# A two-layer attention and feed-forward trunk on one core: products moved behind the conditioning transposes, a table copied by heads, row loads shifted, two small additions moved

## The chip, the core and the metric

The kernel runs on one core of a Trainium2 chip. A core has five engines with a queue each: PE (TensorE, the matrix unit, with PEld as its weight loads), DVE (VectorE), ACT (ScalarE), POOL (GpSimd) and SP (SyncE), which here issues all data transfers. Each engine takes its queue in order; the engines wait for one another by semaphores. Matmul results go to PSUM, eight banks of 2 KB in each of 128 partitions; everything else lies in SBUF. The metric is the device time of one launch in microseconds (us).

## The reference, cut to what matters

One inference step for 1024 prompt rows and 8 groups of 16 sample rows (1152 rows, width 1024), all in float32. Layer 0 has windowed attention with a sink per head and a T5 bias; its output stream gives one key and value projection, which layer 1 uses in banded attention with a bias clipped by distance. Each sub-layer is modulated by a conditioning vector and closed by a LayerNorm.

```
for l in range(2):
    sh_m, sc_m, g_m, sh_f, sc_f, g_f = split(silu(c) @ w_ada[l] + b_ada[l], 6)
    h = x * (1 + sc_m) + sh_m
    if l == 0:
        q, k, v = split(h @ w_qkv_a)              # 16 heads, 4 of keys
        m = max(max(s), sink); e = exp(s - m)     # s = q k / 8 + t5 bias, in the window
        p = e / (sum(e) + exp(sink - m))
    else:
        q = h @ w_q_b                             # k, v: from the stream after layer 0
        p = softmax(q k / 8 + relclip bias)       # band of 9 chunks
    x = LN(ALPHA * x + (1 + g_m) * (p v @ w_o))
    u = (x * (1 + sc_f) + sh_f) @ w_up            # 1024 -> 5632, causal convolution of width 3
    x = LN(ALPHA * x + (1 + g_f) * ((gelu(g) * a) @ w_down))
    if l == 0:
        k_b, v_b = split((x * (1 + sc_kv) + sh_kv) @ w_kv_b)
```

Outputs are the stream, the new keys and values, and the last convolution rows.

## The kernel before

Float32 precision comes from splitting: each operand is held as a rounded high part and the rest as a low part, and each product is three matmuls (low by high, high by low, high by high). `split` (L165, L176) makes the two parts: a cast on ACT, a subtraction on DVE or POOL. `wload` issues the load of a weight block (L180) and splits it into a ring `wring` of four slots `(wh, wl)`, of which attention uses two. `HX` holds the split activations.

The code is written in program order, and a scheduler in the framework orders each engine's queue when the kernel is built, by its own model of the costs; `issue_after(i)` keeps what stands under it from being ordered ahead of the instruction i. So a small edit can reorder whole stages.

The stages of the profile: the opening with the key projections (0 to 70 us), attention 0 (to 420), out projection 0 (to 550), up projection 0 (to 1071), down projection 0 (to 1375), keys and values for layer 1 (to 1570), attention 1 (to 1930), out projection 1 (to 2091), up 1 (to 2560), down 1 (to 2780), and the last norms.

*Opening* (`opening`). The conditioning product has two halves h of 512 columns: 32 matmuls L249 for each, with the weight `adaw` loaded in eight pieces a half; L262 adds the bias, L265 transposes, L268 to L271 copy the result as scale G and shift B. Then each half of x (`x1in`, three blocks of 384 rows) is modulated (L278 on DVE, L280 on ACT), split into HX, and multiplied with the matching half of two key weights, `wk[0]` and `wk[1]` (`mmT`, L376, 12 matmuls for a block, half and weight, 144 in all), which sum up in banks 0 to 5. `tables` makes the T5 table (L1421 on PE, L1422 on DVE, L1423 to DRAM as `ea`), and `skew(0)` copies it into `ska` (L1441), from which shifted bias rows are read (L541, L602).

*Attention.* Scores (L624, L627), softmax (L590 to L603), transposes of the probabilities into a bank of a ring `tbk` of two (L650), whose result ACT casts (L655) and DVE subtracts from (L656), then values (L669 to L681). `sums` makes the row sums of a pair of heads: in layer 0 an exponential of sink minus maximum (L690, ACT), an addition (L691, DVE), a reciprocal (L692), a transpose into a bank of the same ring (L694) and a copy (L695). `item_scores` does the same for sample rows (L769, L770). POOL multiplies (L706) and makes the low parts of weights (L176). For layer 1 `load_hm` loads nine tiles of the stream, modulates them on ACT (L895) and splits them, as input of the query weights (`qload`, `qblock`, L376).

*Down projection* (`down_phase`). 1152 rows are done in three groups of three tiles. For each group a loop over 22 steps j loads one block of the down weight (`in_wdn`, 0.5 MB, L180) and 384 columns of the stored activation (`actD`, L1365), and does 18 matmuls of 512 columns (L1329). Beside the steps, `consts(j)` loads in the first group what the closing norms need: norm rows (L910), gates (L904, L906), and in layer 0 also the second bias table (`tables_b`, to DRAM as `eb`) and `skew(1)`, which copies it 16 x 128 times, shifted, into `skb` (L1441). `resid` loads a tile of the residual stream (L996) at three steps of each group.

## Time and profile before

| | us |
|---|---|
| three runs | 2854.53, 2857.62, 2864.55 |
| median | 2857.62 |
| profiled execution | 2855.29 |
| its span | 2853.2 |

The profile is of one execution; its span runs from the first to the last instruction seen. In a row of the timeline or the chain stand the start, the duration, the engine, the line (L12 is line 12), the operation with output and input, a count, and in brackets the idle time of the engine before it and what ended that. In a row of windows stand, after the stretch, the busy time of PE, PEld, DVE, ACT and POOL with counts, the granted TensorE clock (1.00 is full), the share of the DMA engines in use and their GB/s.

The clock and the transfers over the span, in 40 slices of 71 us:

```profile
PEclk9999989999999999999999999999999999999999
DMA  8655432343444449766785466683232222238652
GB/s 319 186 146 176 112 123 105 102 137 128 140 142 147 143 138 295 250 199 215 264 284 172 121 152 184 172 254 104 89 102 73 70 81 78 77 116 271 224 202 77
```

The digits are tenths. Transfers are heaviest in the opening and in the two down projections (slices 16 to 20 and 37 to 39).

### The profile page before, as it was taken

To read this page: it belongs to the slowest core of one execution; us is meant where nothing else is said; L and a number is where in the kernel's file an instruction comes from. 1 tells how busy PE (TensorE), PEld (TensorE's weight loads), DVE (VectorE), ACT (ScalarE), POOL (GpSimd) and SP (SyncE) were. 2 spreads that over 40 slices of the span, in tenths; PEclk is the share of its full clock that TensorE was granted. 3 is DMA by queue.
4 is the path that set the end of the run, shared out by engine and by line. 5 is a ranking of instruction groups with operands and counts; after the bars stand their busy time and mean duration, and the time that the engine had idled before them with its cause. 6 is when DMAs were issued, how large, how long until landed. Compare 5 with 4: busy or idle time off the path is not lost.

```text
span 2853.2 us, 48907 instructions
## 1 busy us (share of the span) xinstructions
PE 2718.7 (95%) x18086; PEld 2429.6 (85%) x18086; DVE 1681.1 (59%) x3846; ACT 1405.6 (49%) x2996; POOL 1065.2 (37%) x1086
## 2 busy tenths in 40 slices
PE   7998889899999999899999999988999999999998
PEld 5986668899899998788999888866799999997886
DVE  4465657755555555665312677764876555566764
ACT  3465543554444443545424666663455545554441
POOL 0122336676565540000550121131877666630000
PEclk9999989999999999999999999999999999999999
DMA  8655432343444449766785466683232222238652
GB/s 319 186 146 176 112 123 105 102 137 128 140 142 147 143 138 295 250 199 215 264 284 172 121 152 184 172 254 104 89 102 73 70 81 78 77 116 271 224 202 77
DMA packets 215631, 454.48 MB, mean 159 GB/s; under 512 B 39040, under 2 KB 115024, under 8 KB 215392
## 3 DMA queue, kind: packets, MB, share of 16 engines
q1 hardware_dynamic: 215392, 451.35, 49.5%
q8 instruction: 143, 2.34, 0.3%
q14 instruction: 96, 0.79, 0.1%
HBM read 359.40 MB, written 101.30 MB: 161 GB/s over the span
## 4 chain that ended last, share of the span: by engine, by line
PE 64%; DVE 6%; issue 6%; DMA 5%; POOL 2%; ACT 2%; SPq 0%; POOLq 0%; DVEq 0%; ACTq 0%
PE PS L1178 33%; PE PS L1329 15%; PE PS L376 7%; PE PS L388 2%; PE PS L669 1%; PE PS L311 1%; PE PS L650 1%; DMA ws<-in_wdn_dram 1%; POOL HX L176 1%; DMA ws<-in_wo_dram 1%; PE PS L624 1%; DVE F L590 1%; PE PS L627 1%; DVE HX L176 0%; DVE x1att L176 0%
## 5 line engine op out<-in xcount | busy, mean ns | idle before, releaser
L176 POOL TENSOR_TENSOR wl<-ws,wh 128x512 fp32r<-128x512 f32 (+1 forms) x217 | 324.8, 1501 | 649.6 <-ACT wh L165 618.8
L1232 DVE SCALAR_TENSOR_TENSOR PS<-F,PS 128x512 f32<-128x512 f32 (+2 forms) x704 | 348.1, 515 | 141.0 <-ACT PS L1239 62.6
L1178 PE MATMUL PS<-HX,wh 128*128 128x288 f32 x2616 | 402.6, 297 | 12.7 <-DVE F L1027 10.9
L165 ACT CAST wh<-ws 128x512 fp32r<-128x512 f32 (+1 forms) x321 | 244.9, 768 | 316.6 <-PE PS L1329 91.1
L1178 PEld LDWEIGHTS PS<-HX,wh 128*128 128x128 f32 x2616 | 365.7, 189 | 21.4 <-DVE F L1027 11.4
L1329 PE MATMUL PS<-wh,HX 128*128 128x512 f32 x1164 | 363.8, 391 | 8.3 <-DVE HX L176 8.3
L1329 PEld LDWEIGHTS PS<-wh,HX 128*128 128x128 f32 x1164 | 218.9, 188 | 54.4 <-DVE HX L176 9.2
L1178 PE MATMUL PS<-HX,wl 128*128 128x288 f32 x1536 | 253.8, 297 | 0.5 <-ACT F L1202 0.5
L376 PE MATMUL PS<-HX,wh 128*128 128x384 f32 x1248 | 244.6, 339 | 0.0
L1329 PE MATMUL PS<-wl,HX 128*128 128x512 f32 x582 | 227.3, 391 | 0.6 <-DVE wl L176 0.6
L1178 PEld LDWEIGHTS PS<-HX,wl 128*128 128x128 f32 x1536 | 220.0, 188 | 7.1 <-issue 6.2
L376 PEld LDWEIGHTS PS<-HX,wh 128*128 128x128 f32 x1248 | 217.6, 189 | 3.9 <-issue 1.8
L388 PE MATMUL PS<-wh,HX 128*128 128x256 f32 (+1 forms) x936 | 172.0, 314 | 14.6 <-ACT wh L165 7.8
L1178 PE MATMUL PS<-x1att,wh 128*128 128x288 f32 x1168 | 182.2, 297 | 1.6 <-DVE x1att L176 1.6
L1239 ACT ACTIVATE PS<-F 128x512 f32<-128x512 f32 x176 | 138.1, 785 | 74.5 <-DVE F L1211 61.9
L165 ACT CAST HX<-F 128x384 fp32r<-128x384 f32 (+3 forms) x232 | 135.3, 602 | 74.8 <-PE PS L1329 15.6
L1178 PEld LDWEIGHTS PS<-x1att,wh 128*128 128x128 f32 x1168 | 163.9, 188 | 7.0 <-issue 4.9
L706 POOL TENSOR_TENSOR F<-F,gatt 64x512 f32<-64x512 f32 x62 | 79.4, 1281 | 234.9 <-DVE F L681 199.0
L176 DVE TENSOR_TENSOR HX<-F,HX 128x384 fp32r<-128x384 f32 (+3 forms) x188 | 135.4, 731 | 39.1 <-ACT HX L165 36.5
L388 PEld LDWEIGHTS PS<-wh,HX 128*128 128x128 f32 x936 | 135.9, 194 | 25.7 <-ACT wh L165 8.3
L1329 PE MATMUL PS<-HX 128*128 128x512 f32 x630 | 147.7, 394 | 4.8 <-ACT HX L165 4.8
L376 PE MATMUL PS<-HX,wl 128*128 128x384 f32 x624 | 133.4, 351 | 14.5 <-DVE HX L167 8.7
(244 smaller groups left out, 5517.9 us busy)
## 6 DMA issues: line engine op xcount, KB each, us to landing
F<-in_adaw_dram SPq DMA_DIRECT2D x112, 512.0 KB
ws<-in_wup_dram SPq DMA_DIRECT2D x92, 512.0 KB
ws<-in_wdn_dram SPq DMA_DIRECT2D x88, 512.0 KB
actD<-F SPq DMA_DIRECT2D x44, 576.0 KB
F<-actD SPq DMA_DIRECT2D x132, 192.0 KB
F<-in_wdn_dram SPq DMA_DIRECT2D x44, 512.0 KB
x1att<-kH SPq DMA_DIRECT2D x60, 256.0 KB
xd<-F SPq DMA_DIRECT2D x27, 512.0 KB
```

What stands on the lines that cost most here:

```text
L165: self.lastact = nc.scalar.copy(out, in_).ins
L176: self.eng(el).tensor_sub(lo, src, hi.bitcast(F32))
L311: mm = nc.tensor.matmul(ps[32 * j : 32 * j + 32, hf * 256 : hf * 256 + 256], self.cT[:, k * 32 : k * 32 + 32], w[n][:, j * 256 : j * 256 + ...
L376: self.nc.tensor.matmul(out, w[a][:, k * 128 : k * 128 + 128], self.Hx(p, k, s0, n), start=i == 0, stop=i == 23)
L388: self.nc.tensor.matmul(out[:, 0:n], H[:, t0 // 128, p, j * kn + k, :], w[a][:, k * n : k * n + n], start=i == 0, stop=i == 23,)
L590: nc.vector.tensor_tensor_reduce(out=p[:, c0 : c0 + w], in0=ps, in1=b, scale=1.0, scalar=init, op0=ALU.add, op1=ALU.min, accum_out=nm)
L624: mm = nc.tensor.matmul(o, q, khi[a][:, kc], start=first, stop=False, **kw)
L706: self.eng("v" if last else "p").tensor_mul(on[r, q], on[r, q], rb[r, :])
L1178: nc.tensor.matmul(out, w[f][a][:, k * 128 : k * 128 + 128], x[:, k, :], start=start and i == 0, stop=i == 11, skip_group_check=True,)
L1232: nc.vector.scalar_tensor_tensor(o, v, w(i), o, op0=ALU.mult, op1=ALU.add)
L1239: nc.scalar.activation(yp, u[:, bl, 2:258], AF.Identity, bias=w(3), scale=w(2))
L1329: nc.tensor.matmul(ps, h[p][:, i * 128 : i * 128 + 128], w[q][:, hf * 512 : hf * 512 + 512], start=j == 0 and k == 0, stop=j == NFF - 1 an ...
```

## The change

Five edits. (1) In the opening the 36 matmuls of the first half with `wk[1]` are no longer written beside those of `wk[0]`, but behind the second half's transposes, with `issue_after` on the last of these. (2) In layer 1 the ring of two weight slots and the load of the first query weight are put ahead of `load_hm`, and the splits of tiles 4 to 8 there are kept behind that weight's cast. (3) In `sums` the bank is taken at the start, the exponential goes into columns 128 to 131 of it, and the addition reads it from there. (4) In `item_scores` the addition is an activation with bias on ACT. (5) In `down_phase` the steps of `consts` are shifted by 2 (layer 0) or 5 (layer 1), the residual rows are loaded at steps 10, 12 and 14, and the skewed table is copied head by head, one at each of the first 16 steps of the second group.

```diff
@@ -262,7 +262,7 @@
             nc.vector.tensor_add(row[:, cs], ps[:, cs], row[:, 512 + 256 * h : 768 + 256 * h])
             for c in range(2):
                 o = (2 * h + c) * 128
-                nc.tensor.transpose(pt[:, o : o + 128], row[:, o : o + 128], self.ident)
+                tr = nc.tensor.transpose(pt[:, o : o + 128], row[:, o : o + 128], self.ident)
             src = pt[:, cs].rearrange("p (c v j r) -> p v j c r", c=2, v=2, j=2)
             for v in range(2):
                 nc.vector.tensor_copy(aT[:, v, h], src[:, v, :, :, 0:9])
@@ -282,8 +282,15 @@
                     )
                     e = "a" if c % 3 == 2 else "v"
                     self.split(self.tiles(x3[:, c, :]), self.Hx(0, c, s0, w), self.Hx(1, c, s0, w), e, "v")
-                for c in range(2):
-                    self.mmT(wk[c], self.bank(3 * c + bi), s0, w, h)
+                if h == 0:
+                    self.mmT(wk[0], self.bank(bi), s0, w, 0)
+                elif bi == 0:
+                    with self.tc.issue_after(tr.ins):
+                        for b, (z0, z) in enumerate(BLK):
+                            self.mmT(wk[1], self.bank(3 + b), z0, z, 0)
+                if h:
+                    for c in range(2):
+                        self.mmT(wk[c], self.bank(3 * c + bi), s0, w, 1)
         return wk
 
     def ada(self, gi, bank, ring):
@@ -506,6 +513,11 @@
             return 8 * (c // 4) + 4 * a + c % 4 if l == 0 else 2 * c + a
 
 
+        qw = {}
+
+        def qload(c):
+            qw[c] = self.wload(I[("wq0", "wq1")[l]][c])
+
         kvb = Ring(list(SB[l]))
         ka = Arena(self.F, (9504, 0)[l])
         kvt = Ring([(self.X2[:, i * 768 : i * 768 + 768], ka.take(384)) for i in (0, 3, 1, 4)])
@@ -526,9 +538,12 @@
             self.rescale(8, zr)
             for q in range(1, 4):
                 self.vproj(1, q, kvb, kvt)
+            self.wring = Ring(self.wslots[0:2])
+            qload(0)
             self.load_hm(Ring([pall[:, i * 1024 : i * 1024 + 1024] for i in range(3)]), self.affine(4, (8, 9), 1))
 
-        self.wring = Ring(self.wslots[0:2])
+        if l == 0:
+            self.wring = Ring(self.wslots[0:2])
         sbt = []
         base = E[0:1, :]
         for p in range(2):
@@ -577,11 +592,6 @@
                 nc.vector.scalar_tensor_tensor(
                     qs(c, a, o, s0, m), src, -SCALE, hi.bitcast(F32), op0=ALU.mult, op1=ALU.subtract
                 )
-
-        qw = {}
-
-        def qload(c):
-            qw[c] = self.wload(I[("wq0", "wq1")[l]][c])
 
         def softmax(pieces, p, n, sink, nm, rs):
 
@@ -686,11 +696,11 @@
 
             hh = 2 * x.head.c + x.head.a
             cs = slice(hh * 8 + 2 * x.g - 2, hh * 8 + 2 * x.g + 2)
+            t = self.bank(tbk.next())
             if l == 0:
-                nc.scalar.activation(M[:, cs], M[:, cs], AF.Exp, bias=self.sinkH[:, hh : hh + 1])
-                nc.vector.tensor_add(L[:, cs], L[:, cs], M[:, cs])
+                nc.scalar.activation(t[:, 128:132], M[:, cs], AF.Exp, bias=self.sinkH[:, hh : hh + 1])
+                nc.vector.tensor_add(L[:, cs], L[:, cs], t[:, 128:132])
             nc.vector.reciprocal(L[:, cs], L[:, cs])
-            t = self.bank(tbk.next())
             nc.tensor.transpose(t[0:4, 0:128], L[:, cs], self.ident)
             nc.vector.tensor_copy(rl[0:4, :], t[0:4, 0:128])
             q0 = (x.g // 2) * 512
@@ -767,7 +777,7 @@
             if l == 0:
                 e = self.sm.next()[:, 0:1]
                 nc.scalar.activation(e, sink, AF.Exp, bias=nm, scale=-1.0)
-                nc.vector.tensor_add(rs, rs, e)
+                nc.scalar.activation(rs, e, AF.Identity, bias=rs)
             nc.vector.reciprocal(rs, rs)
 
         nk = P0 // 128
@@ -839,7 +849,8 @@
 
         for a in range(2):
             kload(0, a)
-        qload(0)
+        if l == 0:
+            qload(0)
         for bi in range(3):
             qblock(0, bi, qw[0])
         items = [item(p, s) for p in range(2) for s in range(8)]
@@ -884,7 +895,7 @@
         self.nc.sync.dma_start(self.xd[1][t * 128 : t * 128 + 128, :], z)
 
     def load_hm(self, ring, aff):
-        nc = self.nc
+        nc, lead = self.nc, self.lastact
         G, B = aff
         for t in range(NT):
             s = ring.next()
@@ -895,7 +906,10 @@
                     nc.scalar.activation(s3[:, c, :], s3[:, c, :], AF.Identity, bias=B[:, c, 0:1], scale=G[:, c, 0:1])
             else:
                 self.sample_affine(s3, s3, G, B, 0, 8, "v")
-            self.split(s3, self.H[:, t, 0], self.H[:, t, 1], "a", "v")
+            with ExitStack() as es:
+                if t >= 4:
+                    es.enter_context(self.tc.issue_after(lead))
+                self.split(s3, self.H[:, t, 0], self.H[:, t, 1], "a", "v")
 
 
     def ln_gate(self, l, i, smp):
@@ -1367,8 +1381,11 @@
             self.split(r, *h, "a", "v")
             return w, h
 
+        late = 5 if last else 2
+
         def consts(j):
             nonlocal aff
+            j -= late
             if j in (2, 3):
                 self.ln_row(l, 0, j - 2, (ga, ba)[j - 2])
             elif j == 5:
@@ -1380,10 +1397,8 @@
                 self.ln_gate(l, 1, j == 8)
             elif j in (10, 11):
                 self.ln_row(l, 1, j - 10, (self.lng, self.lnb)[j - 10])
-            elif j == 12 and not last:
+            elif j == 13 and not last:
                 self.tables_b(F[0:16, 2048:3072], F[0:16, 3072:4096])
-            elif j == 14 and not last:
-                self.skew(1)
 
         for g, ts in enumerate(GRP):
             final = g == len(GRP) - 1
@@ -1396,7 +1411,9 @@
                 with self.tc.issue_after(self.lastload), self.tc.issue_after(self.lastact):
                     if g == 0:
                         consts(j)
-                    if j in (6, 10, 14):
+                    elif g == 1 and not last and j < 16:
+                        self.skew(1, j, 1)
+                    if j in (10, 12, 14):
                         xs.append(resid(ts[len(xs)]))
                 if todo and j % 4 == 3:
                     finish(*todo.pop(0))
@@ -1435,11 +1452,12 @@
         nc.scalar.copy(t[:, 0:511], t[:, 511:512].to_broadcast([16, 511]))
         nc.sync.dma_start(self.eb, t)
 
-    def skew(self, l):
+    def skew(self, l, h=0, n=16):
         e, sk, w = ((self.ea, self.ska, 384), (self.eb, self.skb, 768))[l]
-        src = e[0:1, :]
+        src = e[h : h + 1, :]
         self.nc.sync.dma_start(
-            sk.rearrange("h (q w) -> h q w", w=w), bass.AP(src.tensor, src.offset, [[w, 16], [0, 128], [1, w]])
+            sk[h : h + n].rearrange("h (q w) -> h q w", w=w),
+            bass.AP(src.tensor, src.offset, [[w, n], [0, 128], [1, w]]),
         )
 
     def build(self):
```

In the opening, PE's queue before, from the first half's products (L376) to the second half's conditioning product (L249), its transposes (L265), the table's product (L1421) and the second half's first products:

```order
L376 MATMUL PS<-HX,wl 128x384 x4
L376 MATMUL PS<-HX,wh 128x384 x8
L376 MATMUL PS<-HX,wl 128x384 x4
L376 MATMUL PS<-HX,wh 128x384 x16
L376 MATMUL PS<-HX,wl 128x384 x4
L376 MATMUL PS<-HX,wh 128x384 x8
L249 MATMUL PS<-F,C 32x256 x20
L265 MATMUL PS<-C,F 128x128 x2
L1421 MATMUL PS<-F 16x384
L376 MATMUL PS<-HX,wl 128x384 x9
```

And PE's queue at the same place after the change (L383 is L376 there, L1438 is L1421):

```order
L383 MATMUL PS<-HX,wh 128x384
L249 MATMUL PS<-F,C 32x256 x4
L383 MATMUL PS<-HX,wh 128x384 x7
L249 MATMUL PS<-F,C 32x256 x16
L265 MATMUL PS<-C,F 128x128 x2
L383 MATMUL PS<-HX,wl 128x384 x4
L383 MATMUL PS<-HX,wh 128x384 x8
L383 MATMUL PS<-HX,wl 128x384 x4
L383 MATMUL PS<-HX,wh 128x384 x8
L383 MATMUL PS<-HX,wl 128x384 x4
L383 MATMUL PS<-HX,wh 128x384 x8
L383 MATMUL PS<-HX,wl 128x384 x7
```

Before, 44 products stand right ahead of the last 20 L249; after, eight of them are still ahead or between, and the 36 of the second key weight follow the transposes.

In down 0, SP's queue before, at the end of the first group (`ws` and `F` take the weight's blocks, `actD` the activation):

```order
L1436 DMA eb<-F 16x768
L1365 DMA F<-actD 128x384
L180 DMA ws<-in_wdn_dram 128x1024
L1365 DMA F<-actD 128x384
L1441 DMA skb<-eb 2048x1x768
L180 DMA F<-in_wdn_dram 128x1024
L1365 DMA F<-actD 128x384
L180 DMA ws<-in_wdn_dram 128x1024
L1365 DMA F<-actD 128x384
```

And SP's queue after the change, in the second group (L1379 is L1365 there, L1458 is L1441):

```order
L180 DMA ws<-in_wdn_dram 128x1024
L1379 DMA F<-actD 128x384
L1458 DMA skb<-eb 128x1x768
L180 DMA F<-in_wdn_dram 128x1024
L1379 DMA F<-actD 128x384
L1458 DMA skb<-eb 128x1x768
L180 DMA ws<-in_wdn_dram 128x1024
L1379 DMA F<-actD 128x384
L1458 DMA skb<-eb 128x1x768
L180 DMA ws<-in_wdn_dram 128x1024
```

One transfer of 2048 rows of 768 has become 16 of 128 rows, each behind one step's two loads; the others follow in the same way.

In down 1, SP's queue before, ahead of the first steps' loads (`x1dn` takes rows; `xd` is the residual stream, `gd` the gates):

```order
L180 DMA ws<-in_wdn_dram 128x1024
L996 DMA x1dn_24120<-xd_95 128x1024
L906 DMA x1dn_24120<-gd 128x1024
L904 DMA x1dn_24120<-gd 128x1x1024
L180 DMA F<-in_wdn_dram 128x1024
L1254 DMA out_conv_dram<-F 128x198
L1365 DMA F<-actD 128x384
L996 DMA x1dn_24120<-xd_95 128x1024
L180 DMA ws<-in_wdn_dram 128x1024
L1365 DMA F<-actD 128x384
L180 DMA ws<-in_wdn_dram 128x1024
```

And SP's queue after it (L1010 is L996, L920 is L906, L1268 is L1254):

```order
L180 DMA ws<-in_wdn_dram 128x1024
L180 DMA F<-in_wdn_dram 128x1024
L1268 DMA out_conv_dram<-F 128x198
L1379 DMA F<-actD 128x384
L1010 DMA x1dn_24135<-xd_95 128x1024
L180 DMA ws<-in_wdn_dram 128x1024
L1379 DMA F<-actD 128x384
L920 DMA x1dn_24135<-gd 128x1024
L1010 DMA x1dn_24135<-xd_95 128x1024
L180 DMA ws<-in_wdn_dram 128x1024
L180 DMA F<-in_wdn_dram 128x1024
```

The two gate loads (L906, L904) and one of the two residual rows no longer stand ahead of the second weight load into `ws` here; one residual row does, and a gate and the other row come behind it.

## The prediction

> **What bounds the kernel now.** I read the page first: the busy shares and the chain that ended last.
>
> ```profile
> PE 2718.7 (95%) x18086; PEld 2429.6 (85%) x18086; DVE 1681.1 (59%) x3846; ACT 1405.6 (49%) x2996; POOL 1065.2 (37%) x1086
> ...
> PE 64%; DVE 6%; issue 6%; DMA 5%; POOL 2%; ACT 2%; SPq 0%; POOLq 0%; DVEq 0%; ACTq 0%
> ```
>
> TensorE (PE) is busy 95% of 2853.2 us, so no stage can be made much shorter by an engine other than PE. The diff adds and removes no matmul. What it can win is part of the 134 us in which PE is idle, and of the time in which PE runs at a lower granted clock after an idle. So I looked for the PE gaps next to the edits, in the timeline, and asked of each gap what ended it.
>
> **Opening.** The timeline of PE, with DVE and SP where they matter, and three windows (us; PE, PEld, DVE, ACT, POOL busy; granted clock; DMA share; GB/s):
>
> ```profile
> 33.87 0.62 PE L249 MATMUL PS<-F,C 128*32 128x256 f32 x2
> 37.13 2.79 PEld L376 LDWEIGHTS PS<-HX,wh 128*128 128x128 f32 x16
> 42.25 2.37 PE L249 MATMUL PS<-F,C 128*32 128x256 f32 x40
> 44.68 0.42 DVE L262 TENSOR_TENSOR F<-PS,F 128x256 f32<-128x256 f32 x1 [12.18 <-PE PS L249]
> 45.98 0.81 PE L1421 MATMUL PS<-F 32*16 32x384 f32 x2 [0.39 <-DVE C L268]
> 48.50 1.01 PE L376 MATMUL PS<-HX,wl 128*128 128x384 f32 x2 [1.70 <-DVE HX L167]
> 48.92 0.64 SPq L1441 DMA_DIRECT2D ska<-ea  x1
> 59.47 0.54 DVE L176 TENSOR_TENSOR HX<-x1in,HX 128x384 fp32r<-128x384 f32 x1
> 59.82 7.61 PE L376 MATMUL PS<-HX,wh 128*128 128x384 f32 x43
> 63.24 1.42 SPq L541 DMA_DIRECT2D F<-ska  x2
> 81.91 0.89 SPq L602 DMA_DIRECT2D F<-ska  x2
> 106.88 0.22 PE L624 MATMUL PS<-x1att 128*128 128x128 f32 x1
> ...
> 0.00:38.00 38.00, 24.74 (x139) 13.09 (x140) 16.63 (x32) 11.79 (x19) 3.08 (x7) 1.00 0.97 377
> 48.00:60.00 12.00, 8.58 (x31) 7.06 (x32) 12.00 (x23) 8.17 (x15) 0.00 (x0) 0.61 0.83 253
> 70.00:120.00 50.00, 49.90 (x367) 48.33 (x366) 13.65 (x43) 17.15 (x47) 7.75 (x7) 1.00 0.68 206
> ```
>
> The second half's 20 conditioning products (L249, the row counts each twice, x40) stand behind 44 L376 products and start at 42.25; their sum is taken by L262 at 44.68. Everything of the second half of x hangs on that: from 48 to 60 PE works 8.58 of 12 us at clock 0.61, while DVE is busy all 12. The data were there long before: 377 GB/s for 38 us are 14.3 MB, which is all that is requested up to there (two halves of the conditioning weight 8.39 MB, x 4.72, two key weights 1.05, small ones 0.13); the x half that comes last is 2.36 MB, some 6 us at that rate, so the weight is in at about 32 to 34.
>
> After the change 8 of the 44 products stay ahead and 36 go behind. A product takes 2.79 / 16 = 0.174 us, an L249 2.37 / 20 = 0.12. From 34.0: 8 x 0.174 + 20 x 0.12 puts L262 at 37.9, **6.8 us earlier**. DVE prepares until 60.0 now, 15.3 us behind L262, so until 53.2 then. PE fills this with the 36 moved products (to about 45), then has 72 of the second half, 12.5 us. Their floor is 57.5; the last block's 24 products behind the last cast end at 53.2 + 4.2 = 57.4. Now they end at 59.82 + 7.61 = 67.4. So the gain lies between the pure shift, 6.8, and 10. PE is busy 49.90 of the 50 us that follow, so the shift goes on into attention 0. What it costs: the skewed table's product (L1421) falls behind 14 products of the second half, to 48 or 50 from 46; the copy, issued at 48.92 and first read at 63.24 (at most 14.3 us), is then issued at 52 to 54 and in by 68. Loads with a score behind them (L602) go out at 81.91 now, near 74 then: 6 us of slack. If that cover were gone, up to 3 us of the 6.8 would go. I take **-8, range -4 to -10**.
>
> **Two additions in attention 0.** The answers for their lines (durations in ns, min/median/max), a stretch of the DVE and POOL timelines, what PE waited for at the transposes of probabilities, L650 (us, times), and the stage as a window:
>
> ```profile
> L691 DVE TENSOR_TENSOR F<-F x32: 142/163/2262, 114.8 to 389.1; 128x4 f32<-128x4 f32 x32
> L770 DVE TENSOR_TENSOR C<-C x16: 140/157/2075, 190.2 to 391.1; 128x1 f32<-128x1 f32 x16
> L681 DVE TENSOR_TENSOR F<-PS,gatt x128: 381/417/420, 122.0 to 1961.6; 64x256 f32<-64x256 f32 x128
> L690 ACT ACTIVATE F<-F,C x32: 281/292/300, 114.1 to 388.6; 128x4 f32<-128x4 f32 x32
> L692 DVE RECIPROCAL F<-F x32: 156/178/179, 115.0 to 389.9; 128x4 f32<-128x4 f32 x32
> ...
> 372.28 2.26 DVE L691 TENSOR_TENSOR F<-F 128x4 f32<-128x4 f32 x1
> 372.17 2.36 POOL L176 TENSOR_TENSOR x1att<-ws,x1att 128x1024 fp32r<-128x1024 f32 x1 [3.42 <-ACT x1att L165]
> ...
>   DVE wh L656: 18.2, 20
>   DVE HX L656: 12.7, 24
> ...
> 110.00:420.00 310.00, 280.67 (x2127) 226.79 (x2125) 196.12 (x671) 180.16 (x536) 84.52 (x82) 0.94 0.47 140
> ```
>
> An addition of 4 columns that takes 163 ns as a rule takes 2262 at worst, and the one-column one 2075; L681, which has one input in PSUM, never passes 420 in 128 runs. The longest starts at 372.28 and ends with POOL's addition, at 374.54 and 374.53. L691 stays on DVE but reads PSUM; L770 goes to ACT, as an activation like L690, 0.29 us (16 x 0.29 = 4.7 us on an engine busy 180 of 310 us). What DVE gets back is bounded by the single rows: over the median of each line, six of the 32 (0.54 to 2.26 us) are 5 us too long, five of the 16 (0.33 to 2.08) are 4; none of it shows if PE has other work then. PE is 91% busy in this stage; I take a third, **-3, range -9 to 0**.
>
> For L691 to read PSUM, the bank is taken before the exponential instead of behind the reciprocal: held longer by 0.292 + 0.163 + 0.178 = 0.63 us, 32 times, 20 us of holding. Those banks are the ones that PE waits for at L650: 30.9 us by the two rows, over both attentions. The ends are 0, if nothing else wants the bank, and +20, if each is paid. Behind the exponential on ACT are casts of the next scores; they are waited for by DVE's L656, then PE. The 44 waits are 0.70 us each; PE has other independent products in its queue most of the time. I take three more such waits, **+2, range 0 to +20**.
>
> **Attention 1's start.** ACT's casts ahead of the first query weight's, and the wait behind it:
>
> ```profile
> 1561.76 1.06 ACT L165 CAST HX<-F 128x1024 fp32r<-128x1024 f32 x1
> ...
> 1566.33 1.06 ACT L165 CAST wh<-ws 128x1024 fp32r<-128x1024 f32 x1
> 1569.87 2.93 PE L376 MATMUL PS<-HX,wl 128*128 128x384 f32 x8 [4.33 <-POOL wl L176]
> ```
>
> PE waits 4.33 us for the low part of the weight that this cast feeds. This cast of a tile on ACT, 1.06 us, and the one before it go behind the weight's: up to 2.1 us earlier. PE then reaches the third block, whose tiles the moved casts make later: **-1.5, range -4 to +3**. The scheduler also orders the rest of both attentions anew; I find no reason for a sign there, and leave 3 us each way in the range.
>
> **Down 0.** The chain of waits, SP's and PE's timeline and two windows:
>
> ```profile
> 1099.80 25.86 PE PS L1329 x114
> ...
> 1120.92 0.61 SPq L1441 DMA_DIRECT2D skb<-eb  x1
> ...
> 1132.18 16.07 DMA ws<-in_wdn_dram
> ...
> 1149.44 0.80 PE L1329 MATMUL PS<-wh,HX 128*128 128x512 f32 x1 [7.48 <-DVE HX L176]
> 1153.46 0.39 PE L1329 MATMUL PS<-wl,HX 128*128 128x512 f32 x1
> ...
> 1130.00:1145.00 15.00, 11.96 (x53) 9.58 (x51) 0.00 (x0) 0.00 (x0) 0.00 (x0) 1.00 1.00 311
> 1163.00:1240.00 77.00, 77.00 (x353) 63.97 (x352) 54.24 (x81) 42.08 (x74) 0.00 (x0) 1.00 0.69 231
> ```
>
> The skewed table is one copy of 16 x 128 x 768 x 4 bytes = 6.29 MB. The weight load issued 11 us behind it takes 16.07 us, the DMA engines are full, ACT and DVE get nothing for 15 us, and PE stands for 7.48 us, then starts 10 matmuls in 4.0 us, to 1153.46, where 25.86 / 114 = 0.227 us each would be 2.3. At 311 GB/s the copy is 20 us of transfer ahead of that load; with it gone the load lands long before it is needed. That is 7.5 + 1.7 = 9.2 us, on the chain. I take **-8.5**, as the row loads, moved in the same group from step 6 to 10, now arrive later beside it.
>
> The 16 pieces (0.39 MB) come one a step in the second group of tiles. A step is 18 matmuls, 4.1 us. From 1163 to 1240 231 GB/s are 17.8 MB; with the copy it is 24.1 MB, 313 GB/s over the same 77 us. That is what the engines moved when full (311), so the second group just fits. If the rate were 280, it would be 9 us short, less the loads ahead: range of the whole **-9 to 0**. SP queues each piece behind that step's loads, and the piece's source is written long before, so it holds nothing up there. Its readers stand in attention 1, hundreds of us later.
>
> A rule of the Trainium skill speaks against the split, DMA: Bandwidth & Descriptors, section Bandwidth: transfers should be gathered to 1 MiB or more for three quarters of the peak. Its table has 1 MB at 341 GB/s and 64 KB at 138; an estimate between them for 0.39 MB is some 270, by which the second group would come out 12 us short. The trace doesn't bear this out: many loads of 0.5 MB in flight moved 377 GB/s in the opening's first 38 us. It stays as a rival.
>
> **Down 1.** The gap at its start:
>
> ```profile
> 2567.05 13.04 DMA ws<-in_wdn_dram
> ...
> 2581.22 9.79 PE L1329 MATMUL PS<-HX 128*128 128x512 f32 x31 [4.77 <-ACT HX L165]
> ...
> 2560.00:2581.00 21.00, 15.85 (x75) 12.77 (x73) 14.83 (x25) 10.78 (x16) 0.51 (x3) 0.97 0.89 255
> ```
>
> PE waits 4.77 us for a weight load that takes 13.04 us, then runs 31 matmuls in 9.79 us, where 31 x 0.227 are 7.0: 2.7 us more. Ahead of that load stand, beside weights, two residual rows and two gate loads; the change moves the gates and one row, 1.5 MB, behind it. At 255 GB/s that is 5.9 us, over the 4.77. Part of the slow clock remains, since other loads stay tight: **-5, range -7 to 0**.
>
> **Sum.** -8 - 3 + 2 - 1.5 - 8.5 - 5 = -24 against the profiled execution's 2855.3 (span 2853.2 and 2.1 around it), 2831.3. The median of the three runs is 2857.6, 2.3 above, so **2833.5**, put down as 2833.
>
> **The rivals.**
> 1. *The opening gives nothing.* The first scores wait for table, bias or keys, and the 8 us come back as an idle of PE in 70 to 120 or at the first L624. Against it: 6 us of slack above. Then 2841.5.
> 2. *The pieces stall the second group.* What down 0 wins returns as gaps of L1329 between 1165 and 1240, or the rate stays near 280. Then 2842. The skill's rule goes in this direction, and by its estimate it would be some 2846.
> 3. *The split or the later rows do not reach their gap.* In down 1 the load that PE waits for could be late by its own queue: then its 5 us stay, 2838. This is inside the forecast's range.
> 4. *Slower: the bank.* ACT takes its work in order. If each exponential waits until the bank's last readers (a cast and a subtraction, at L655 and L656) are through, everything behind it on ACT, the next casts among it, is late by that wait. The 44 waits of 0.70 us give the size, with the 0.63 of longer holding 1.33 us a sum, 32 x 1.33 = 43 us. All of it on PE's path would make 2833.5 - 2 + 43 = 2874.5; it decides from 26 / 32 = 0.8 us a sum. For it: these banks are where PE waits at L650 already. Against it: ACT is idle 130 of 310 us there, and can make up a late cast.
>
> **Chances.** The forecast, with all terms inside their ranges (2820 to 2838), 0.60; rivals 1 and 2, 0.14 and 0.11 (around 2842); a bank that costs a part, 5 to 20 us, 0.09 (2838 to 2853); slower by the bank, 0.06. The ends: all terms at their best, -10 - 9 - 4 - 9 - 7 - 6 = -45, do not come together; I go to -38, 2820, less 2 for spread, 2818. Upwards it takes in rivals 1 and 2 with a part of the bank: 2848. A measurement of this kernel tells 0.3%, 8.6 us, from no change, so faster means under 2849: the forecast, both rivals and part of the third case, 0.87. Same 0.07, slower 0.06.
>
> **What will show it.** In the changed profile: L262 near 38 and L376 of the opening over near 58 to 61; the first L624 near 99 in place of 106.9; no row of L702 (the addition, now with PSUM) far over 0.2 us; ACT's idle before the exponential small; no PE gap over 2 us at L1329 between 1100 and 1160, and a DMA share near 1 with PE full in the second group; the gap at down 1's start under 1 us. I am wrong if attention 0 is longer than before from its first score to out_proj, or if new gaps stand in the second group of down 0.

## The result, and the profile after

Five runs of the changed kernel have a median of 2833.22 us (2828.17 to 2843.35), against 2861.19 for the kernel before in five (the three above and two more, 2854.53 to 2865.44). The ratio is 0.9912, with a 95% interval of 0.9898 to 0.9926: 0.9% faster. The profiled execution's span went from 2853.2 to 2826.4 us, 26.8 less.

The page of the changed kernel, busy time and share of the chain:

```profile
PE 2706.6 (96%) x18086; PEld 2419.6 (86%) x18086; DVE 1666.8 (59%) x3830; ACT 1411.4 (50%) x3012; POOL 1068.2 (38%) x1086
...
PE 77%; DMA 7%; DVE 6%; issue 4%; ACT 3%; POOL 2%; SPq 0%; POOLq 0%; DVEq 0%; ACTq 0%
```

The 18086 matmuls are the same; PE's busy time fell by 12.1 us, and since the work is the same, that part is mostly matmuls that ran at a higher clock. To see where the rest went, take from PE's timeline the start of the first matmul of each stage in both kernels. What lies between two marks is the length of the stage (a down projection is counted to the start of its last matmul):

| stage, from PE's timeline | before | after | difference |
|---|---|---|---|
| start to the first score | 106.9 | 99.7 | -7.2 |
| attention 0 and out projection 0 | 409.4 | 399.3 | -10.1 |
| up 0 | 555.0 | 554.5 | -0.5 |
| down 0 | 285.1 | 275.6 | -9.5 |
| keys and values of layer 1 | 213.5 | 213.2 | -0.3 |
| attention 1 and out projection 1 | 488.0 | 495.8 | **+7.8** |
| up 1 | 503.9 | 504.0 | +0.1 |
| down 1 | 277.5 | 270.0 | -7.5 |

*Opening.* The timeline of the changed kernel, DVE and PE, and the window from 48 to 60:

```profile
38.21 0.42 DVE L262 TENSOR_TENSOR F<-PS,F 128x256 f32<-128x256 f32 x1 [5.41 <-PE PS L249]
...
38.88 0.95 PE L383 MATMUL PS<-HX,wl 128*128 128x384 f32 x4
...
47.77 0.81 PE L1438 MATMUL PS<-F 32*16 32x384 f32 x2
...
99.68 0.22 PE L634 MATMUL PS<-x1att 128*128 128x128 f32 x1
...
48.00:60.00 12.00, 12.00 (x72) 11.49 (x71) 8.12 (x15) 3.47 (x8) 0.00 (x0) 1.00 0.62 204
```

The bias is added at 38.21, 6.5 us earlier, and behind the transposes PE goes on at 38.88 with the moved products. From 48 to 60 it is busy all 12 us at full clock, where it was busy 8.58 at 0.61. The 144th product of the opening ends at 60.5 (67.4 before).

*Down 0 and down 1.* The chain of waits from 1080 to 1160, the first steps of down 1 in PE's timeline, and two windows:

```profile
1079.95 80.24 PE PS L1343 x354
...
2541.94 0.86 PE L1343 MATMUL PS<-wh,HX 128*128 128x512 f32 x3
2547.26 0.50 PE L1343 MATMUL PS<-wl,HX 128*128 128x512 f32 x1 [0.60 <-DVE wl L176]
...
1144.40:1236.80 92.40, 92.40 (x421) 76.81 (x420) 61.49 (x90) 47.62 (x81) 0.00 (x0) 1.00 0.76 270
2541.00:2562.00 21.00, 20.40 (x94) 16.71 (x93) 17.30 (x31) 11.56 (x17) 0.51 (x3) 1.00 0.83 264
```

For 80 us the chain in down 0 is PE alone, 354 matmuls of 0.227 us: no wait for a load is left. The second group takes the pieces at 270 GB/s, with a DMA share of 0.76 and PE never idle. At down 1's start the longest wait is 0.60 us, and the clock stays at 1.00.

*Attention 1.* The start, where PE now waits twice:

```profile
1538.71 1.03 ACT L165 CAST wh<-ws 128x1024 fp32r<-128x1024 f32 x1
...
1542.24 2.93 PE L383 MATMUL PS<-HX,wl 128*128 128x384 f32 x8 [3.78 <-POOL wl L176]
1556.12 0.33 PE L634 MATMUL PS<-x1att 128*128 128x128 f32 x1 [2.99 <-DVE x1att L592]
```

### The profile page after: what moved, and what is told of

It is laid out like the page before. It is cut to its first block, busy times and chain, and to the rows that moved or that the text cites. A ratio compares the mean times of both kernels' runs of the same rounds, so it can differ in the third digit from the quotient of the medians.

```text
span 2826.4 us, 48889 instructions
## 1 busy us (share of the span) xinstructions
PE 2706.6 (96%) x18086; PEld 2419.6 (86%) x18086; DVE 1666.8 (59%) x3830; ACT 1411.4 (50%) x3012; POOL 1068.2 (38%) x1086
## 3 DMA queue, kind: packets, MB, share of 16 engines
q1 hardware_dynamic: 215632, 451.35, 49.4%
## 4 chain that ended last, share of the span: by engine, by line
PE 77%; DMA 7%; DVE 6%; issue 4%; ACT 3%; POOL 2%; SPq 0%; POOLq 0%; DVEq 0%; ACTq 0%
PE PS L1192 33%; PE PS L1343 16%; PE PS L383 11%; PE PS L395 7%; DMA F<-in_adaw_dram 3%; PE PS L679 2%; PE PS L318 2%; PE PS L660 2%; PE PS L634 1%; DMA ws<-in_wo_dram 1%; DVE F L600 1%; PE PS L637 1%; DMA ws<-oN 1%; ACT HX L165 1%; POOL HX L176 1%
## 5 line engine op out<-in xcount | busy, mean ns | idle before, releaser
L383 PE MATMUL PS<-HX,wh 128*128 128x384 f32 x1248 | 246.7, 340 | 0.0
L383 PEld LDWEIGHTS PS<-HX,wh 128*128 128x128 f32 x1248 | 218.1, 190 | 5.8 <-issue 3.5
L395 PE MATMUL PS<-wh,HX 128*128 128x256 f32 (+1 forms) x936 | 172.8, 315 | 18.8 <-ACT wh L165 9.0
L395 PEld LDWEIGHTS PS<-wh,HX 128*128 128x128 f32 x936 | 136.5, 194 | 29.8 <-ACT wh L165 9.4
L1343 PEld LDWEIGHTS PS<-HX 128*128 128x128 f32 x630 | 118.2, 188 | 24.6
```

The costliest lines, as they stand in the source:

```text
L383: self.nc.tensor.matmul(out, w[a][:, k * 128 : k * 128 + 128], self.Hx(p, k, s0, n), start=i == 0, stop=i == 23)
L395: self.nc.tensor.matmul(out[:, 0:n], H[:, t0 // 128, p, j * kn + k, :], w[a][:, k * n : k * n + n], start=i == 0, stop=i == 23,)
L1343: nc.tensor.matmul(ps, h[p][:, i * 128 : i * 128 + 128], w[q][:, hf * 512 : hf * 512 + 512], start=j == 0 and k == 0, stop=j == NFF - 1 an ...
```

## The experiments

Each kernel in the table has one profile, and its stages are read from it as above. How much such a reading is worth shows in kernels whose queues are the same in a stage. The down projections then agree within 0.1 us where no load is late, and within 2.4 where the loads stand as before (down 0 took 285.1, 284.3 and 286.7 us with the same queues). The up projections agree within 2.5. Attention 0 spreads by 4 us in six of seven profiles with the changed kernel's queues, and the seventh is 11 above the shortest; attention 1 took from 487.4 to 492.8 us with the same queues. All lengths in us, marks as in the table above:

| kernel | to first score | attention 0 | down 0 | attention 1 | down 1 | span |
|---|---|---|---|---|---|---|
| before | 106.9 | 409.4 | 285.1 | 488.0 | 277.5 | 2853.2 |
| changed | 99.7 | 399.3 | 275.6 | 495.8 | 270.0 | 2826.4 |
| changed, repeated | 101.4 | 397.9 | 275.6 | 494.9 | 270.0 | 2823.6 |
| without attention 1's edit | 99.9 | 395.3 | 275.6 | 490.3 | 270.0 | 2818.3 |
| the same, timed | 98.8 | 406.0 | 275.6 | 487.4 | 270.0 | 2823.7 |
| tiles 5 to 8 held | 100.9 | 397.0 | 275.6 | 488.3 | 270.0 | 2819.1 |
| old opening | 107.9 | 408.5 | 275.6 | 490.9 | 270.0 | 2837.9 |
| one copy | 100.4 | 397.4 | 287.2 | 493.7 | 270.0 | 2835.1 |
| old row loads | 100.8 | 397.5 | 275.7 | 497.0 | 277.1 | 2834.3 |
| old row-sum addition | 99.4 | 407.1 | 275.6 | 496.7 | 270.0 | 2834.0 |
| old sample-row addition | 99.8 | 404.8 | 275.6 | 493.3 | 270.0 | 2828.1 |
| before, new opening alone | 100.1 | 410.5 | 284.3 | 493.2 | 275.5 | 2851.1 |
| before, new row-sum addition alone | 107.4 | 405.2 | 286.7 | 490.2 | 276.6 | 2850.7 |
| before, new down projections alone | 106.8 | 411.2 | 275.6 | 492.8 | 270.0 | 2841.2 |

### The table as one copy

```diff
+            elif j == 14 and not last:
+                self.skew(1)
...
-                    elif g == 1 and not last and j < 16:
-                        self.skew(1, j, 1)
```

> The changed kernel with the skewed table as one copy again, at step 16 of the first group (two steps later than before). Theory A, the copy's 20 us of transfers ahead of the weight loads make the gap: down 0 is 7 to 10 us longer by its second third than in the changed kernel, with a gap of PE of 5 to 8 us. Theory B, it was the row loads' shift that mended down 0: then it is under 3 us longer. Down 1 is unchanged by both.

Down 0 is 287.2 us, 11.6 longer, and nothing else moves beyond the spread. SP's and PE's timeline and the chain of this kernel:

```profile
1111.32 0.61 SPq L1458 DMA_DIRECT2D skb<-eb  x1
1112.34 6.62 SPq L180 DMA_DIRECT2D ws<-in_wdn_dram  x1
...
1140.25 0.79 PE L1343 MATMUL PS<-wh,HX 128*128 128x512 f32 x1 [8.69 <-DVE HX L176]
...
1120.43 18.63 DMA F<-in_wdn_dram
```

Theory A, with both sizes a little over its ranges: a load behind the copy takes 18.63 us, and PE stands for 8.69. The gain of down 0 belongs to the copy; the row loads' shift, which is still in this kernel, does not mend it. That the loss is 11.6 and the gain 9.5 may come from the place, since the copy stands two steps later here than before; no run tells.

### Old row loads

```diff
-        late = 5 if last else 2
+        late = 0 if last else 0
...
-            elif j == 13 and not last:
+            elif j == 12 and not last:
...
-                    if j in (10, 12, 14):
+                    if j in (6, 10, 14):
```

> The changed kernel with the norm rows, gates and residual rows loaded at their old steps in both down projections; the table's copy stays in 16 pieces. Theory A: down 1 is 7 to 8 us longer in its first third, with the gap of 4 to 5 us back, and down 0 is the same within 1 us. Theory B: the gap in down 1 came from the phase in which the stage begins, and stays away: under 2 us. Theory C: the shift helped down 0 too: over 2 us there.

PE's timeline at down 1's start:

```profile
2561.59 9.95 PE L1343 MATMUL PS<-HX 128*128 128x512 f32 x31 [4.18 <-ACT HX L165]
```

Down 1 is 277.1 us, 7.1 longer, with the gap (4.18) and the 31 slow matmuls back; down 0 is 275.7, unchanged. Theory A; B and C fall.

### The edits of the down projections alone, in the kernel before

```diff
+        late = 5 if last else 2
...
-            elif j == 14 and not last:
-                self.skew(1)
...
+                    elif g == 1 and not last and j < 16:
+                        self.skew(1, j, 1)
-                    if j in (6, 10, 14):
+                    if j in (10, 12, 14):
```

> The kernel before with only the edits of the down projections (table in pieces, row loads shifted). Theory A, the parts add up: down 0 is 8.5 to 11 us shorter and down 1 6.5 to 8 us, together 15 to 19, with nothing else that changes by over 3 us. Theory B, down 1's gap hangs on what comes ahead: under 4 us there. Attention 0's queues are those of before: the last piece of it (PE work from 225 to 250 us in the count of matmuls at their full-speed length) takes 48 to 52 us at a granted clock under 0.85 if the order sets the clock there (before 50.9 at 0.78, the changed kernel 43.3 at 1.00); if the clock falls by chance in each execution, it may come out anywhere from 43 to 52.

Down 0 is 9.5 us shorter and down 1 7.5, 17.0 together: the two parts stand by themselves. The span fell by only 12.0, since attention 1 came out 4.8 longer in this profile, 3.8 of it behind the last scores, where PE's queue differs from before in some 50 rows. That is more than the 3 us expected, but the same queues took 490.3 and 487.4 us in the two profiles without attention 1's edit (below), so much of it is spread. On the last piece of attention 0 see below; the 43.3 us of the expectation is another cut of that piece, which with the cut used below is 44.4.

### Old opening; new opening alone

```diff
-                if h == 0:
-                    self.mmT(wk[0], self.bank(bi), s0, w, 0)
-                elif bi == 0:
-                    with self.tc.issue_after(tr.ins):
...
+                for c in range(2):
+                    self.mmT(wk[c], self.bank(3 * c + bi), s0, w, h)
```

> The changed kernel with the second key weight's first-half products put back beside the first's. Theory A: the opening gives 7 to 9 us, and only there: first score 7 to 9 us later, and the first up product later by as much, 7 to 9. Theory B: the other 10 us that the changed kernel wins in attention 0 hang on the opening's order too; then the first up product comes 15 us later or more. Theory C: they were won in spite of it, and attention 0 takes up most of the 7 to 9: first up product under 4 us later. The down projections are as in the changed kernel within 1 us.

> The kernel before with only the opening changed. Theory A: the first score is 7 to 8 us earlier than before, and the first up product 7 to 9 us. Theory B: the first up product is 15 us earlier or more, as undoing this part alone suggests (17.1 of 17.8 us were lost). Theory C: order decides in the rest of attention 0, with either sign: the first score 7 to 8 us earlier, the first up product anywhere from 0 to 18. Down 0 and down 1 are as before within 1 us.

Undone, the first score is 8.2 us later and attention 0 9.2 longer, 17.4 together: theory B by its number. Alone, the first score is 6.8 us earlier and attention 0 1.1 longer. The first up product is 5.7 us earlier then, under theory A's 7 to 9, and down 1 came out 2.0 shorter with the queues of before, which is spread. The opening's worth in its own stage, 7 to 8 us, is shown: the ten profiles with the new opening have the first score at 98.8 to 101.4 us, the four with the old one at 106.8 to 107.9. That it does anything in attention 0 is not shown: by itself it gives nothing there, and the 9.2 us of the kernel with the old opening lie within the 11 by which equal queues differ.

### The two additions

```diff
-            t = self.bank(tbk.next())
             if l == 0:
-                nc.scalar.activation(t[:, 128:132], M[:, cs], AF.Exp, bias=self.sinkH[:, hh : hh + 1])
-                nc.vector.tensor_add(L[:, cs], L[:, cs], t[:, 128:132])
+                nc.scalar.activation(M[:, cs], M[:, cs], AF.Exp, bias=self.sinkH[:, hh : hh + 1])
+                nc.vector.tensor_add(L[:, cs], L[:, cs], M[:, cs])
             nc.vector.reciprocal(L[:, cs], L[:, cs])
+            t = self.bank(tbk.next())
```

> The changed kernel with the addition of the row sums put back: bank taken behind the reciprocal, exponential and addition in SBUF. Theory A: the stretched additions come back on DVE (some 5 us in six or so of 32), and attention 0 is 1 to 5 us longer than in the changed kernel at the first up product. Theory B: the bank held longer cost more than that; then attention 0 is shorter by over 2 us. Theory C: neither is felt, and the new order of attention 0, which this edit alone also brings, decides with either sign, by more than the 5 us that DVE can give. The opening and the down projections are unchanged.

The sample rows' addition back on DVE:

```diff
-                nc.scalar.activation(rs, e, AF.Identity, bias=rs)
+                nc.vector.tensor_add(rs, rs, e)
```

> The changed kernel with the sample rows' addition back on DVE. Theory A: up to 4 us of stretched additions return on DVE; attention 0 is 0 to 4 us longer. Theory C: the order decides, with either sign, by more than 4 us. The rest is unchanged.

And the first of the two edits, the other way round, in the kernel before:

> The kernel before with only the row sums' addition reading PSUM, its bank taken first. Theory A: attention 0 is 1 to 5 us shorter at the first up product, the opening unchanged. Theory B (the bank): longer by over 2 us. Theory C (order): either sign, over 5 us. No addition of this line takes over 0.25 us by A and C alike; if one does, reading PSUM isn't what shortens it.

The additions' lines (min/median/max in ns) in the kernel with the old row sums, in the one with the old sample rows, in the changed kernel and in the one with the old opening:

```profile
L701 DVE TENSOR_TENSOR F<-F x32: 141/164/1390, 106.1 to 380.2; 128x4 f32<-128x4 f32 x32
```

```profile
L780 DVE TENSOR_TENSOR C<-C x16: 148/159/1772, 191.7 to 377.5; 128x1 f32<-128x1 f32 x16
```

```profile
L702 DVE TENSOR_TENSOR F<-F,PS x32: 126/155/160, 106.3 to 388.8; 128x4 f32<-128x4 f32 x32
```

```profile
L695 DVE TENSOR_TENSOR F<-F,PS x32: 127/152/159, 115.3 to 403.2; 128x4 f32<-128x4 f32 x32
```

With an input in PSUM no addition takes over 0.16 us in any of these kernels, and with two inputs in SBUF the long ones are back. That part is shown. But attention 0 does not follow what they are worth: undone, the row sums cost 7.8 us and the sample rows 5.5, both beyond theory A's range; the row sums alone, in the kernel before, give 4.2, inside it; and both together with the old opening give 0.9 (408.5 against 409.4), although no addition is long there either. So DVE's time alone does not decide. By their numbers the two undone runs are theory C, but each is one profile, and the changed kernel's own queues took up to 406.0.

Where the differences lie is seen in the last heads. Count PE's matmuls at the full-speed interval of their shape; then the piece from 225 to 250 us of that count is the same amount of work in every kernel, some 306 matmuls. As windows: before, the down projections alone, old row sums, old opening, changed, changed once more, and without attention 1's edit in its timed profile:

```profile
338.99:389.91 50.92, 42.95 (x306) 31.11 (x306) 36.95 (x132) 32.35 (x96) 18.70 (x14) 0.78 0.35 107
```

```profile
337.64:390.01 52.37, 45.10 (x307) 33.64 (x306) 36.27 (x131) 32.51 (x96) 18.44 (x13) 0.71 0.34 107
```

```profile
330.31:380.22 49.91, 44.52 (x307) 33.05 (x306) 34.53 (x127) 33.78 (x105) 18.37 (x12) 0.74 0.37 113
```

```profile
336.51:386.64 50.13, 43.93 (x307) 32.11 (x306) 33.84 (x131) 34.05 (x104) 20.46 (x16) 0.76 0.42 124
```

```profile
327.61:372.04 44.43, 35.99 (x306) 24.98 (x306) 33.55 (x131) 33.86 (x104) 20.31 (x14) 1.00 0.45 136
```

```profile
328.94:373.73 44.79, 37.00 (x306) 26.07 (x306) 33.34 (x131) 33.91 (x104) 20.27 (x14) 0.96 0.44 133
```

```profile
329.56:378.54 48.98, 42.69 (x306) 30.95 (x306) 33.68 (x131) 33.98 (x104) 20.23 (x14) 0.79 0.41 122
```

The same work takes 44 to 45 us at a granted clock of 0.96 to 1.00, and 49 to 52 at 0.71 to 0.79. PE's idle time in it hardly differs: 8.0 us before, 8.4 in the changed kernel. The profiles of the changed kernel and of those kernels whose queues are the same in attention 0 are seven: six have the high clock (0.89 to 1.00, 44.1 to 45.3 us), one, the last above, fell to 0.79 and took 49.0; with its out projection its attention 0 is 406 us. The two with the queues of before have 0.78 and 0.71. Of the three kernels not shown, the one with the new row sums alone has 0.92 and 45.4 us, the one with the new opening alone 0.71 and 52.2, the one with the old sample rows 0.79 and 49.4. So the order of the queues seems to set the clock in this piece, and chance has a part in it, as the seven show; how much is order isn't shown, since most orders have one profile.

### Attention 1's edit: without it, and with tile 4 let go

Without it, the first query weight stands behind the tiles again, and no split is held:

```diff
-            self.wring = Ring(self.wslots[0:2])
-            qload(0)
             self.load_hm(
...
-            with ExitStack() as es:
-                if t >= 4:
-                    es.enter_context(self.tc.issue_after(lead))
-                self.split(s3, self.H[:, t, 0], self.H[:, t, 1], "a", "v")
+            self.split(s3, self.H[:, t, 0], self.H[:, t, 1], "a", "v")
```

> The changed kernel with the load of layer 1's first query weight and the splits of its tiles put back as before; the rest stays changed. In the changed kernel attention 1 falls back by 7.7 us against before (from the first query product to the first up product: -27.6 to -19.9). Theory A: the splits of tiles kept behind the weight's cast come too late for the third block of query products; then the idle before the first score (2.99 us) goes, and the stage is 4 to 8 us shorter than in the changed kernel. Theory B: the scheduler's new order of the rest of attention 1, or transfers, cost it; then the start changes by under 1 us and the stage is no shorter by over 2 us. Stages ahead of it are as in the changed kernel within 1 us by both; if not, that is the spread of one profile.

Attention 1 is 490.3 us, 5.5 shorter than in the changed kernel, and the idle of 2.99 us before the first score is gone. Of the 8.1 us by which its span is shorter, 4.0 lie in attention 0, where its queues are the changed kernel's: spread. So it was timed, beside a second form that holds only the splits of tiles 5 to 8:

```diff
-                if t >= 4:
+                if t >= 5:
```

> The changed kernel without the edit of attention 1, timed: 2822 to 2829 by the profiles (8.1 us less, of which 3 lie in an attention 0 with the same queues and are spread), ratio to before 0.986 to 0.990. If the start of attention 1 is a matter of spread, it is the changed kernel's time again, 2833.

> The changed kernel with the splits of tiles 5 to 8, and not 4 to 8, kept behind the weight's cast. Theory A, tile 4 alone makes the third block late: as without the edit, 2822 to 2829, or 1 us better for the earlier weight. Theory B, any hold of those splits costs: near 2833.

> The changed kernel once more, beside the two above on the same chip: 2829 to 2836. Its attention 0 has the clock near full in its last piece, 43 to 45 us, if the order sets it; 48 or more if that was luck.

The three were timed on the same chip (five, four and five runs), against 2854.82 us for the kernel before (nine runs):

| | median, us | ratio to before, 95% |
|---|---|---|
| changed | 2831.93 | 0.9915 (0.9902 to 0.9929) |
| without attention 1's edit | 2822.01 | 0.9880 (0.9865 to 0.9895) |
| tiles 5 to 8 held | 2822.79 | 0.9888 (0.9874 to 0.9902) |

Both beat the changed kernel, by 9.9 and 9.1 us in the medians, and both lie inside the 2822 to 2829 expected: theory A, it is the hold of tile 4 that costs. The changed kernel came out as expected too, with 44.8 us in the last piece of attention 0. The loads of the tiles of the stream show how; SP's timeline, first of the changed kernel, then of the one with tiles 5 to 8 held:

```profile
1543.29 0.33 SPq L902 DMA_DIRECT2D F<-hmD  x1
...
1544.43 0.32 SPq L902 DMA_DIRECT2D F<-hmD  x1
```

```profile
1535.88 0.32 SPq L902 DMA_DIRECT2D F<-hmD  x1
...
1543.12 0.32 SPq L902 DMA_DIRECT2D F<-hmD  x1
```

`load_hm` has three buffers, so tile 7 is loaded into the one that tile 4 leaves. Held behind the weight's cast (1538.71), tile 4 leaves it late, tile 7's load goes out at 1543.29 in place of 1535.88, and the last tiles, of which the third block consists, come late: PE does two blocks, waits 2.99 us, and its clock falls (0.87 from 1539 to 1577, 0.96 with tile 4 let go).

```profile
1539.00:1577.00 38.00, 31.07 (x156) 28.87 (x157) 23.57 (x55) 23.50 (x48) 8.18 (x3) 0.87 0.36 115
```

```profile
1539.00:1577.00 38.00, 33.34 (x190) 31.38 (x191) 26.58 (x67) 26.68 (x57) 7.98 (x3) 0.96 0.46 142
```

Counted by the same work, the changed kernel has lost some 5 us against before when the start is over (some 4 in its repetition), and some 3 more over the next 100 us of work, in both profiles alike. The kernel with the old opening has tile 4 held as well, loses some 4 at the start and nothing over that stretch: its queues there are nearly those without the edit. So somewhat more than half is the late tiles, and the rest the other order that the scheduler made of what follows.

## Why the prediction was right, point by point

The forecast of 2833 met 2833.22. That it met it so closely is luck: two of its terms were wrong by 9 us each, with opposite signs. Also, the median before rose by 3.6 us from three runs to five, so that the measured gain is 28.0 us where 24 were forecast. Three terms, the opening and the two down projections, were right in mechanism and near in size; together they make 24.2 of the profile's 26.8 us.

- **Opening, -8:** -7.2 in the profile, -6.8 alone, 8.2 when undone. The steps held: L262 at 38.21 (37.9 worked out), PE dense until the end, and the table's later product cost nothing. The end of the 144 products came at 60.5, near the pure shift's 60.6 and not the 57.4 of the floor: the first value projections (L395) now run among them.
- **Additions, -3, and the bank, +2:** attention 0 with its out projection gave -10.1. The stretched additions were read rightly and are gone. The bank was sized from the wrong stage: the two rows below, PE's waits at the transposes over both attentions, are 30.9 us before and 33.9 in the changed kernel (28.1 in its repetition), but in attention 0 alone they are 1.9, 5.1 and 1.8. The rest stands in attention 1, whose sums have no exponential. So no run shows the +2, nor the 0.70 us a wait from which the slower rival, up to 43 us, was worked out, and that rival did not come. What is seen of it is 4.2 us in which ACT waits for the bank's last readers ahead of the exponentials, in the changed kernel and in its repetition, and none before. What the step missed is the granted clock in the last heads: it priced only DVE's time, and left the slow stretches there (0.78) as they were. Of the 10.1 us, 6.5 are the last piece (50.9 to 44.4), at the clock of 1.00. Why the clock stayed up is open, as said above. The rows, of the changed kernel:

```profile
  DVE HX L666: 17.2, 31
  DVE wh L666: 16.7, 16
```

- **Attention 1's start, -1.5, and its new order, no sign:** +7.8, outside the -4 to +3 of that term even with the 3 us for the order, which make it +6. The step counted the two casts that move behind the weight's, and named the later tiles of the third block, but not the load that waits for tile 4's buffer. A moved instruction that frees a buffer moves the next load.
- **Down 0, -8.5:** -9.5, and with the copy put back 11.6. The pieces found room in the second group: over its first 77 us, the stretch of the forecast, it is 290 GB/s at a DMA share of 0.80, not the 313 and the share near 1 worked out (270 and 0.76 over all 92 us). A reason may be that loads which caught up there after the stall before were made earlier now; no run tells.
- **Down 1, -5:** -7.5, the whole gap and the whole slow clock behind it. The term was held back for loads that "stay tight"; none did.

Of the rivals, the first did not happen (the first score came 7.2 us earlier), nor the second: the pieces of 0.39 MB cost nothing, so the rule of the Trainium skill that was weighed there (DMA: Bandwidth & Descriptors, section Bandwidth) doesn't decide here, where many loads are in flight. Nor did the third: the gap at down 1's start is 0.60 us.

The parts add up in the down projections and the opening, where each has its own wait. In attention 0 the single profiles don't show that they do: alone, the row sums give 4.2 us, undone they cost 7.8, with a spread of up to 11.

## What to carry to other kernels

Before a large transfer is put into a stage that streams weights, compare its transfer time with the lead of the loads behind it: 20 us of copying ahead of a load issued 10 us before it was needed cost a stall of 7.5 and a slow clock, and the same bytes one piece a step cost nothing. When an instruction is put behind another, ask which buffer it frees and which load waits for that: here a split held for one cast cost more than the cast's gain. And where a scheduler orders the queues, price an edit inside its own wait, and check each part by itself: the changed kernel without one of its five edits is 0.3% faster than with it.

## What the runs showed that was not expected

The granted clock fell in the last heads of attention 0 after quite short idles. Windows of the kernel with the old row sums, then of the changed kernel:

```profile
320.00:324.00 4.00, 2.66 (x27) 1.25 (x23) 2.90 (x10) 3.53 (x11) 2.48 (x2) 0.77 0.64 193
324.00:328.00 4.00, 3.85 (x27) 3.14 (x23) 2.49 (x11) 2.89 (x9) 2.95 (x4) 0.50 0.54 156
```

```profile
332.00:336.00 4.00, 2.45 (x23) 1.61 (x16) 2.99 (x10) 3.86 (x14) 3.39 (x2) 1.00 0.13 48
376.00:380.00 4.00, 2.31 (x19) 1.56 (x18) 0.89 (x3) 1.79 (x3) 2.35 (x2) 1.00 0.12 39
```

In the first, PE is busy 2.66 of 4 us, with one idle of 1.24 us in it, and then runs at 0.50. In the second it is busy less, 2.45 and 2.31, with idles of 1.30 and 1.60, and keeps 1.00. The Trainium skill (TensorE: Matmul & The Clock Gate, Part 1) puts the fall to half clock after an idle window of about 3.4 us that runs freely; no idle here is half as long. Neither one idle's length nor the busy share of 4 us tells from these rows what sets the fall. The traces tell more when they are cut where the clock changes: in all fourteen profiles each state of it, full or half, lasts a multiple of 3.41 us. Of the steps of 3.41 us at full clock, in both attentions with their out projections, 96 of the 100 in which PE was busy for less than 0.55 of the step were followed by a fall, 42 of the 221 between 0.55 and 0.75, and none of the 3077 above. So several short idles in one step can do what a whole idle step does. The middle stays open, and the stretches above lie in it: the step ahead of the fall has 0.61, and one of 0.62 in the changed kernel had none. The clock is worth some 5 to 8 us in the last piece, and by the seven profiles it comes and goes between executions of the same queues.

SP itself is held by the one copy of 2048 rows: the issue of the next load takes 6.62 us, and 5.31 in the kernel before (a load's issue takes 0.33 as a rule).
